# Add and gelu over 1024 x 4096 in fp32: larger rows, three adds on GpSimd, and another order on ScalarE

## The chip, the core and the metric

The kernel runs on one NeuronCore of a Trainium2 chip. The metric is the device time of one execution in microseconds (us). Before the change it was 120.32 us, the median of three runs (120.19 to 120.32).

## The reference

Two fp32 arrays `x` and `y` of 1024 x 4096 are added, and the tanh form of gelu is taken of the sum:

```python
z = x + y
return (0.5 * z * (1 + np.tanh(np.sqrt(2 / np.pi) * (z + 0.044715 * z ** 3)))).astype(np.float32)
```

Each of `x`, `y` and the output has 16.78 MB, so 50.33 MB go through the DMA engines.

## The kernel before

The arrays are seen as 128 partitions with 32768 elements each (L87). The tile `z` (L117) holds all 32768 elements per partition: `x` is loaded into it, the sums overwrite `x`, and the gelus overwrite the sums. The tile `y` (L118) has room for one half, 16384 elements; the second half of `y` goes into the same place as the first. So a load of the second half of `y` has to wait until the adds that read that part of the first half are done.

**Transfers.** All of them are issued by SyncE (SP), in the order of L158 to L160, and run through one queue on 16 DMA engines: the first half of `y`; the two halves of `x`; the second half of `y` in two pieces of 12288 and 4096 elements (`yloads`, L91); the two halves of the output (`stores`, L92). A piece of n elements is moved in 128 rows, one for each partition, of 4n bytes: 64 KB rows for a half, 48 KB and 16 KB rows for the two pieces. `begin_early` puts the first two loads ahead of the barrier with which the program starts. In the text below the transfers are called y1, x0, x1, y2 (with y3 where there is a second piece), store 0 and store 1.

**Work.** The 32768 elements are cut into chunks (L93), 15 of 2048 and at the end two of 1024. For each chunk VectorE adds `z` and `y` (L151), and ScalarE takes the gelu in place (L156). GpSimd and PSUM have no part in it (`by_pool` and `in_psum` are empty, L94 and L95), though the functions `to_psum` and `add` could use them.

**Order.** Lists for each queue (L158 to L166) say what each engine does and in what order; engines run their lists in that order, and waits on semaphores are put in where one operation needs another (`needs`, L168). ScalarE takes the gelus in the order of the chunks. Store 0 needs the gelus of the first half; these are long done when `y` of the second half is still on its way, so L133 to L139 add a wait on add 8 (`GATE = 8`, L96), the first add of the second half. Store 1 needs the gelus of the second half. The wait for store 1's end is the last thing in the program (`wait_late`).

Of the kernel before, what the change touches and what calls it, by code (L numbers as in the profile page):

```python
# [8 lines left out]
def begin_early(nc, count):  # L9


    head, body = (b.instructions for b in nc.main_func.blocks[:2])
    SP = mybir.EngineType.SP
    moved = [i for i in body if i.engine == SP and isinstance(i, mybir.InstDMACopy)][:count]
    assert not any(i.sync_info and i.sync_info.on_wait for i in moved)
    assert all(i.regs_accessed() == ((), ()) for i in moved)
    at = next(k for k, i in enumerate(head) if i.engine == SP)
    for k, i in enumerate(moved):
        body.remove(i)
        head.insert(at + k, i)  # L20


def wait_late(nc):

    body, end = (b.instructions for b in nc.main_func.blocks[1:3])
    last = [i for i in body if isinstance(i, mybir.InstDMACopy)][-1]
    (sem,) = [u.id for u in last.sync_info.on_update]
    all_done = end[0]  # L30
    reset = next(i for i in end if isinstance(i, mybir.InstDrain) and i.is_reset_sema)
    at = end.index(reset)
    clear = end[at + 1]
    first, stop = reset.reset_range_start, reset.reset_range_stop
    assert all_done.engine == mybir.EngineType.SP and reset.engine == mybir.EngineType.Pool
    assert isinstance(clear, mybir.InstISA) and clear.engine == mybir.EngineType.Pool
    waits = all_done.sync_info.on_wait
    (its,) = [w for w in waits if w.id == sem]

    end[0] = mybir.InstDrain(  # L40
        name=all_done.name, engine=all_done.engine, debug=all_done.debug, is_reset_sema=False,
        sync_info=mybir.SyncInfo(on_wait=[w for w in waits if w.id != sem], on_update=[]),
    )
    parts = []
    for f, e in ((first, sem), (sem + 1, stop)):
        if f < e:
            nc.gpsimd.sem_clear(range(f, e))
            parts.append(nc.cur_bb.bb.instructions.pop())
    end[at + 1 : at + 2] = parts
    end.append(  # L50
        mybir.InstEventSemaphore(
            name=clear.name, engine=mybir.EngineType.Activation, debug=clear.debug,
            sync_info=mybir.SyncInfo(
                on_wait=[its],
                on_update=[
                    mybir.SyncUpdate(
                        sync_type="semaphore", id=sem, ant_name=its.ant_name,
                        update_mode="sem-sub-imm", update_value=its.wait_value,
                    )
                ],  # L60
            ),
        )
    )


@with_exitstack
def kernel(
    ctx: ExitStack,
    tc: tile.TileContext,
    x: bass.AP,  # L70
    y: bass.AP,
    out: bass.AP,
):

    nc = tc.nc
    P = nc.NUM_PARTITIONS  # L80
    fp32 = mybir.dt.float32
    act = mybir.ActivationFunctionType

    N, D = x.shape
    assert N % P == 0
    TOT = N // P * D
    xv, yv, ov = (a.rearrange("(p n) d -> p (n d)", p=P) for a in (x, y, out))  # L87

    HALF = TOT // 2
    xloads = [HALF, HALF]  # L90
    yloads = [16384, 12288, 4096]  # L91
    stores = [16384, 16384]  # L92
    chunks = [2048] * 15 + [1024, 1024]  # L93
    by_pool = []  # L94
    in_psum = []  # L95
    GATE = 8  # L96

    def ranges(sizes):
        ends = [sum(sizes[: i + 1]) for i in range(len(sizes))]
        assert ends[-1] == TOT  # L100
        return [(e - f, e) for e, f in zip(ends, sizes)]

    xr, yr, sr, cr = (ranges(r) for r in (xloads, yloads, stores, chunks))
    C = len(cr)
    second = next(c for c in range(C) if cr[c][0] == HALF)

    def over(rs, lo, hi):
        return [i for i, (a, b) in enumerate(rs) if a < hi and b > lo]

    pool_sb = ctx.enter_context(tc.tile_pool(name="xz", bufs=1))  # L110
    pool_y = ctx.enter_context(tc.tile_pool(name="y", bufs=1))
    pool_ps = ctx.enter_context(
        tc.tile_pool(name="ps", bufs=max(1, len(in_psum)), space=bass.MemoryType.PSUM)
    )

    one = pool_sb.tile([P, 992], fp32, tag="one", name="one")
    zt = pool_sb.tile([P, TOT], fp32, tag="z", name="z")  # L117
    yt = pool_y.tile([P, HALF], fp32, tag="y", name="y")  # L118
    xp, adds = {}, {}

    def load_x(i):
        a, b = xr[i]
        nc.sync.dma_start(out=zt[:, a:b], in_=xv[:, a:b])

    def load_y(i):
        a, b = yr[i]
        o = a % HALF
        nc.sync.dma_start(out=yt[:, o : o + b - a], in_=yv[:, a:b])  # L128

    def store(i):  # L130
        a, b = sr[i]
        ins = nc.sync.dma_start(out=ov[:, a:b], in_=zt[:, a:b])
        if i == 0 and GATE is not None:  # L133
            tc.add_manual_dep(
                ins.ins,
                adds[GATE].name,
                mybir.DependencyInfo(mybir.DependencyClass.Sync, mybir.DependencyReason.DATA),
                reason="the stores join the queue when the last load is nearly done",
            )  # L139

    def to_psum(c):
        a, b = cr[c]
        xp[c] = pool_ps.tile([P, 2048], fp32, tag="xp", name=f"xp{c}")
        nc.scalar.copy(out=xp[c][:, : b - a], in_=zt[:, a:b])

    def add(c):
        a, b = cr[c]
        o = a % HALF
        eng = nc.gpsimd if c in by_pool else nc.vector
        first = xp[c][:, : b - a] if c in in_psum else zt[:, a:b]  # L150
        ins = eng.tensor_add(out=zt[:, a:b], in0=first, in1=yt[:, o : o + b - a])  # L151
        adds[c] = ins.ins

    def gelu(c):
        a, b = cr[c]
        nc.scalar.activation(out=zt[:, a:b], in_=zt[:, a:b], func=act.Gelu_apprx_tanh)  # L156

    sp = [(load_y, i) for i in over(yr, 0, HALF)] + [(load_x, 0), (load_x, 1)]  # L158
    sp += [(load_y, i) for i in over(yr, HALF, TOT)]
    sp += [(store, i) for i in range(len(stores))]  # L160
    pool = [(add, c) for c in by_pool]
    dve = [(add, c) for c in range(C) if c not in by_pool]
    order = list(range(second, C))
    acts = [(gelu, c) for c in range(second)] + [(to_psum, c) for c in in_psum]
    acts += [(gelu, c) for c in order]
    assert sorted(order) == list(range(second, C))  # L166

    needs = {  # L168
        load_x: lambda i: [],
        load_y: lambda i: [(add, c) for c in over(cr, yr[i][0] - HALF, yr[i][1] - HALF)],  # L170
        to_psum: lambda c: [(load_x, i) for i in over(xr, *cr[c])],
        add: lambda c: [(load_x, i) for i in over(xr, *cr[c])]
        + [(load_y, i) for i in over(yr, *cr[c])]
        + [(to_psum, k) for k in in_psum if k == c],
        gelu: lambda c: [(add, c)],
        store: lambda i: [(gelu, c) for c in over(cr, *sr[i])]
        + ([(add, GATE)] if GATE is not None else []),
    }
    queues = [sp, pool, acts, dve]
    done = set()  # L180
    with tc.manual_schedule():
        nc.vector.memset(one[:, :1], 0.0)  # L182
        nc.scalar.activation(out=one[:, :1], in_=one[:, :1], func=act.Gelu_apprx_tanh)  # L183
        while any(queues):
            moved = False
            for q in queues:
                while q and all(n in done for n in needs[q[0][0]](q[0][1])):
                    fn, arg = q.pop(0)
                    fn(arg)
                    done.add((fn, arg))  # L190
                    moved = True
                    if q is not sp:
                        break
            assert moved, [q[:1] for q in queues]

    ctx.close()
    tc.close()
    tc.compile()  # L198
    begin_early(nc, 2)
    wait_late(nc)  # L200
# [30 lines left out]
```

## Time and profile before

| What | Value |
|---|---|
| Median of three runs | 120.32 us (120.19 to 120.32) |
| The profiled execution | 120.19 us |
| Its span, from the first to the last instruction | 118.7 us |
| VectorE busy | 35.5 us, 17 adds and one memset |
| ScalarE busy | 32.0 us, 17 gelus, a table load and one small gelu |
| GpSimd busy | 0.2 us, four memsets |
| HBM read and written | 33.55 MB and 16.78 MB, 424 GB/s over the span |

In the tables of the profile, `L151 DVE` is line 151 of the kernel on VectorE; ACT is ScalarE, POOL is GpSimd, SPq is SyncE's queue. `out<-in` names the tiles. The span is shorter than the execution's time by what lies around it, 1.49 us here.

### The profile page before, as it was taken

What the parts mean: (1) busy time and instruction counts of PE and PEld (TensorE: products, weight loads), DVE (VectorE), ACT (ScalarE), POOL (GpSimd) and SP (SyncE); (2) the same over time, 40 slices, a digit from 0 to 9 for tenths busy, and PEclk for the clock granted to TensorE, in tenths of its full rate; (3) what the DMA queues carried; (4) which work ended last, traced back from release to release, by engine and by line L of the source; (5) the groups of instructions that cost most, each with busy time, mean ns of one, the idle gap of its engine ahead of it and who ended that gap; (6) DMA issues with size and microseconds to landing.
All of it is one profiled execution on the core that took longest, in us unless ns stands there. A gap on an engine that the chain in (4) does not pass through costs nothing.

```text
span 118.7 us, 96 instructions
## 1 busy us (share of the span) xinstructions
DVE 35.5 (30%) x18; ACT 32.0 (27%) x19; POOL 0.2 (0%) x4
## 2 busy tenths in 40 slices
DVE  0000000000000099999900000699999300000000
ACT  5000000000000029899850000079989800000000
POOL 0000000000000000000000000000000000000000
DMA  9889888998899888988898996998899889988890
GB/s 353 353 353 685 375 353 353 596 464 353 353 442 618 353 353 353 685 375 353 353 530 381 414 530 271 431 624 353 353 596 464 353 353 442 618 353 353 353 685 22
DMA packets 1008, 50.33 MB, mean 424 GB/s; under 512 B 112, under 2 KB 112, under 8 KB 112
## 3 DMA queue, kind: packets, MB, share of 16 engines
q1 hardware_dynamic: 1008, 50.33, 98.5%
HBM read 33.55 MB, written 16.78 MB: 424 GB/s over the span
## 4 chain that ended last, share of the span: by engine, by line
DMA 52%; DVE 22%; ACT 2%; DVEq 2%; ACTq 1%; SPq 0%; issue 0%
DMA z<-in_x_dram 34%; DVE z L151 22%; DMA y<-in_y_dram 17%; ACT z L156 2%; DVEq L198 2%; ACTq L198 1%; SPq L128 0%; DVEq L151 0%
## 5 line engine op out<-in xcount | busy, mean ns | idle before, releaser
L151 DVE TENSOR_TENSOR z<-z,y 128x2048 f32<-128x2048 f32 (+1 forms) x17 | 35.5, 2160 | 56.2 <-DMA z<-in_x_dram 40.0
L156 ACT ACTIVATE z<-z 128x2048 f32<-128x2048 f32 (+1 forms) x17 | 30.5, 1807 | 61.3 <-DVE z L151 61.3
L183 ACT ACT_TABLE_LOAD x1 | 1.3, 1283 | 1.3 <-PEq L215 1.3
L182 DVE MEMSET one<- 128x1 f32 x1 | 0.1, 59 | 1.3 <-PEq L215 1.3
L183 ACT ACTIVATE one<-one 128x1 f32<-128x1 f32 x1 | 0.2, 203 | 0.0
L215 POOL MEMSET const-bfloat16-1.0<- 128x1 bf16 x1 | 0.1, 101 | 0.0
L215 POOL MEMSET const-uint8-127<- 128x1 uint8 x1 | 0.1, 101 | 0.0
L215 POOL MEMSET const-float32-0.0<- 128x1 f32 x1 | 0.1, 98 | 0.2 <-issue 0.2
L215 POOL MEMSET const-float32-1.0<- 128x1 f32 x1 | 0.1, 98 | 0.0
## 6 DMA issues: line engine op xcount, KB each, us to landing
y<-in_y_dram SPq DMA_DIRECT2D x1, 6144.0 KB, 20.5
y<-in_y_dram SPq DMA_DIRECT2D x1, 2048.0 KB, 20.9
z<-in_x_dram SPq DMA_DIRECT2D x2, 50.1
out_dram<-z SPq DMA_DIRECT2D x2, 22.9
y<-in_y_dram SPq DMA_DIRECT2D x1, 22.0
```

The costliest lines, as they stand in the source:

```text
L151: ins = eng.tensor_add(out=zt[:, a:b], in0=first, in1=yt[:, o : o + b - a])
L156: nc.scalar.activation(out=zt[:, a:b], in_=zt[:, a:b], func=act.Gelu_apprx_tanh)
L182: nc.vector.memset(one[:, :1], 0.0)
L183: nc.scalar.activation(out=one[:, :1], in_=one[:, :1], func=act.Gelu_apprx_tanh)
L198: tc.compile()
L215: nc = _bacc.Bacc("TRN2", target_bir_lowering=False, num_devices=1)
```

## The change

The second half of `y` is loaded in one piece, so all six transfers have 64 KB rows. The wait on add 8 (`GATE`) is gone. The chunks are cut anew: the first half into two of 1024 (chunks 0 and 1) and seven of 2048 (2 to 8), the second half into 512, 1536 (9 and 10), six of 2048 (11 to 16), and 1024, 512, 512 (17 to 19). GpSimd does the adds of chunks 7, 8 and 12. ScalarE copies `x` of chunks 2 to 6 and 9 to 11 into PSUM, into a tile of 4096 elements (two places of 2048, or 512 + 1536 in the first), and VectorE's adds of these chunks take `x` from there; VectorE's other adds read both operands from SBUF as before. ScalarE's list is: the copies of 2 to 6, the gelu of 0, the copies of 9 to 11, then the gelus of 1 to 8, then those of 9, 10, 11, 13, 12, and 14 to 19. The copies of 9 to 11 need x1, and they stand ahead of the gelus of 1 to 8.

```diff
-    yloads = [16384, 12288, 4096]
+    yloads = [16384, 16384]
     stores = [16384, 16384]
-    chunks = [2048] * 15 + [1024, 1024]
-    by_pool = []
-    in_psum = []
-    GATE = 8
+    chunks = [1024, 1024] + [2048] * 7 + [512, 1536] + [2048] * 6 + [1024, 512, 512]
+    copies = {2: 0, 3: 2048, 4: 0, 5: 2048, 6: 0, 9: 0, 10: 512, 11: 2048}
+    on_vector = [0, 1, 2, 3, 4, 5, 6, 9, 10, 11, 13, 14, 15, 16, 17, 18, 19]
+    on_gpsimd = [7, 8, 12]
+    on_scalar = [("copy", c) for c in (2, 3, 4, 5, 6)] + [("gelu", 0)] + [("copy", c) for c in (9, 10, 11)] + [("gelu", c) for c in range(1, 9)] + [("gelu", c) for c in (9, 10, 11, 13, 12, 14, 15, 16, 17, 18, 19)]
...
+    ps = pool_ps.tile([P, 4096], fp32, tag="ps", name="ps")
...
+    def in_psum(c):
+        a, b = cr[c]
+        return ps[:, copies[c] : copies[c] + b - a]
...
     def store(i):
         a, b = sr[i]
-        ins = nc.sync.dma_start(out=ov[:, a:b], in_=zt[:, a:b])
-        if i == 0 and GATE is not None:
-            tc.add_manual_dep(
...
+        nc.sync.dma_start(out=ov[:, a:b], in_=zt[:, a:b])
+
+    def copy(c):
+        a, b = cr[c]
+        nc.scalar.copy(out=in_psum(c), in_=zt[:, a:b])

     def add(c):
         a, b = cr[c]
         o = a % HALF
-        eng = nc.gpsimd if c in by_pool else nc.vector
-        first = xp[c][:, : b - a] if c in in_psum else zt[:, a:b]
-        ins = eng.tensor_add(out=zt[:, a:b], in0=first, in1=yt[:, o : o + b - a])
-        adds[c] = ins.ins
+        eng = nc.gpsimd if c in on_gpsimd else nc.vector
+        first = in_psum(c) if c in copies else zt[:, a:b]
+        eng.tensor_add(out=zt[:, a:b], in0=first, in1=yt[:, o : o + b - a])
...
+    pool = [(add, c) for c in on_gpsimd]
+    dve = [(add, c) for c in on_vector]
+    acts = [(gelu if what == "gelu" else copy, c) for what, c in on_scalar]
...
-        store: lambda i: [(gelu, c) for c in over(cr, *sr[i])]
-        + ([(add, GATE)] if GATE is not None else []),
+        store: lambda i: [(gelu, c) for c in over(cr, *sr[i])],
```

## The prediction

> **What bounds the kernel now.** I read the page first, for who is busy. VectorE and ScalarE are busy for less than a third of the span. The DMA row of the 40 slices is full from end to end, and the one queue holds the 16 engines for 98.5% of the span:
>
> ```profile
> DMA  9889888998899888988898996998899889988890
> ...
> q1 hardware_dynamic: 1008, 50.33, 98.5%
> ```
>
> So time can be won only by moving the bytes in less engine time, and lost wherever an engine is left without a row. Next I asked for stretches of 1 us or less. The last two columns are the share of the 16 engines' time taken by rows that start in the stretch, and GB/s.
>
> ```profile
> 0.00:1.00 1.00, 0.00 (x0) 0.00 (x0) 0.20 (x4) 1.00 0.00 0
> 1.00:1.25 0.25, 0.00 (x0) 0.00 (x0) 0.00 (x0) 1.00 8.84 2884
> 1.25:1.50 0.25, 0.06 (x1) 0.24 (x1) 0.00 (x0) 1.00 2.88 1049
> 1.50:1.80 0.30, 0.00 (x0) 0.30 (x1) 0.00 (x0) 1.00 0.61 218
> ...
> 4.00:5.00 1.00, 0.00 (x0) 0.00 (x0) 0.00 (x0) 1.00 2.42 1049
> ...
> 63.00:64.00 1.00, 0.00 (x0) 0.00 (x0) 0.00 (x0) 1.00 1.82 786
> ...
> 76.00:77.00 1.00, 1.00 (x1) 0.00 (x0) 0.00 (x0) 1.00 1.11 475
> ```
>
> Two things are to be seen. First the **price of a row**: 1049 GB/s in 1 us is 16 rows of 64 KB, each taking 2.42 us; 786 is 16 rows of 48 KB at 1.82; 475 is 29 rows of 16 KB, at 1.11 x 16 / 29 = 0.61. Second the **price of a start**: y1 is issued at 0.00 and nothing moves for 1.00 us; 11 of the 16 engines begin by 1.25 (2884 GB/s x 0.25 us), the last between 1.50 and 1.80.
>
> Last the timeline and the landings give each transfer. Issue to landing is 22.0 for y1. x0 lands at 0.43 + 40.84 = 41.27 (chain of waits), x1 at 1.27 + 59.3 = 60.6, y2 at 54.70 + 20.47 = 75.17, y3 at 59.1 + 20.9 = 80.0. For the stores:
>
> ```profile
> L132 SPq DMA_DIRECT2D out_dram<-z x2: 343/346/348, 77.6 to 94.6; - x2
> ...
> DMA to landing us min/median/max: 21.7/22.9/24.0
> ```
>
> Store 0: 77.6 + 21.7 = 99.3; store 1: 94.6 + 24.0 = 118.6, the end. Between landings a half takes 19.3 us (41.27 to 60.6, 80.0 to 99.3, 99.3 to 118.6). Each transfer is issued well ahead of the landing of the one before it: store 0 by 80.0 - 77.6 = 2.4, store 1 by 99.3 - 94.6 = 4.7. I call this the **lead**. y1, before which nothing ran, took 22.0 - 19.3 = 2.7 more than a half. So a lead of 2.7 should always be enough, and store 0 shows that 2.4 is.
>
> **The change, part by part.**
>
> *Rows.* y2 and y3 give each engine 8 rows of 48 KB and 8 of 16 KB, 8 x (1.82 + 0.61) = 19.44; 8 rows of 64 KB are 8 x 2.42 = 19.36. The gain is 0.08 us, and it lies on the queue, so it counts in full. This is all that the change can win: bytes and engines stay. y2 then lands at 79.9 instead of y3's 80.0. One issue on SP (0.33) goes, hidden behind the queue.
>
> *First half.* VectorE's own row prices the adds, ScalarE's the copies:
>
> ```profile
> L151 DVE TENSOR_TENSOR z<-z,y 128x2048 f32<-128x2048 f32 x15 | 33.2, 2285 | 56.2 <-DMA z<-in_x_dram 40.0 <-DMA y<-in_y_dram 16.2
> L156 ACT ACTIVATE z<-z 128x2048 f32<-128x2048 f32 x15 | 28.6, 1910 | 61.3 <-DVE z L151 61.3
> L151 DVE TENSOR_TENSOR z<-z,y 128x1024 f32<-128x1024 f32 x2 | 2.4, 1219 | 0.0
> L156 ACT ACTIVATE z<-z 128x1024 f32<-128x1024 f32 x2 | 2.0, 1039 | 0.0
> ```
>
> Back to back an add of 2048 comes every 2.20 us (eight take 17.71 in the timeline) and, by the two shapes, 0.15 + 1.04 per 1000 elements; a gelu has 0.17 + 0.85 per 1000, and each of a run starts 0.09 before the last ends (3.80 for 1.91 + 1.04 + 1.04). From x0 at 41.3: VectorE's two adds of 1024 end at 43.7, the first copy at 43.3, and five adds from PSUM at 2.2 each end at 54.8. GpSimd's two adds run beside them. y2 is then issued at 54.9, a lead of 5.7 on x1. No cost. An add with one operand in PSUM and a copy into PSUM are not in the trace; the nearest rows are the same shapes above, which I take, with the fixed part (0.15, 0.17) gone or doubled as bounds.
>
> *Adds on GpSimd.* The trace has none. The floor is VectorE's 2.29. The one operation that both do is the memset of one column, 0.10 on GpSimd and 0.06 on VectorE, a ratio of 1.7, which makes 3.9 for 2048 elements; twice that, 7.8, is my ceiling, if it takes its two operands in turn. I take 3.9, by the row nearest to it. In the second half VectorE adds from PSUM until 84.5, and that covers 4.5 of chunk 12.
>
> The Trainium skill, "GPSIMD Engine Reference", section 3.1, gives 4497 ns for such an add and advises VectorE for elementwise work. By it the add just fits its cover, and the sum stays. No run here shows it yet.
>
> *ScalarE's order, store 0.* The copies of 9 to 11 wait for x1 and hold the gelus of 1 to 8 behind them, and store 0 waits for those. x1 lands at 60.6, ScalarE starts 0.1 later; copies 0.51 + 1.38 + 1.82; gelu 1 0.95; seven gelus 12.72; 0.09 for the last one's end: 78.2. The lead on y2 (79.9) is 1.7, where it was 2.4. Bounds of the copies: 0.5 either way.
>
> *Second half, store 1.* Before, three quarters of the work could start at 75.2. Now all of it starts at 79.9, that is 4.7 later. VectorE: chunk 9 from 80.0 to 80.7, 10 to 82.4, 11 to 84.6, 13 to 86.8, then one every 2.2. ScalarE follows: gelu 9 at 80.8, 10 at 82.4, 11 at 84.6 to 86.55; gelu 13 waits for its add and starts at 86.85; from there it is never without work: 13, 12, 14, 15, 16 at 1.82, 17 at 0.95, 18 at 0.51, and 19 with 0.60 end at 98.0. ScalarE is the later engine (VectorE is done at 95.8). Store 1 is issued at 98.0; without a hole store 0 would land at 99.2. The lead falls from 4.7 to **1.2**.
>
> *What a short lead costs.* This is the disputed price. Say that a store needs a lead L for no hole; then store 1 lands at 98.0 + L + 19.3. Ceiling of L: 2.4, by store 0 before. Floor: 0, if the queue had its rows ready at once. Nearest row: the start of y1, where the last engine got its first row 1.5 to 1.8 after the issue. I take L = 2.1, the middle of 1.8 and 2.4. Then store 1 lands at 119.4. Store 0's own hole (2.1 - 1.7 = 0.4) adds nothing to that, since store 1's issue is later still. The span goes from 118.7 to 119.5 (0.04 from landing to the last instruction), and with 120.19 - 118.7 = 1.49 around it the time is **121.0**. That is against the profiled 120.19; the median, 120.32, is 0.13 higher, which I leave to the range.
>
> The Trainium skill, "DMA: Bandwidth & Descriptors", section "Latency and other measured facts", has about 600 ns to the first byte of a transfer issued from SyncE. The row here is 1.00 to 1.80. With 0.6 in place of L there is no hole and the sum is 120.1.
>
> **Rivals.**
>
> *No hole (not slower).* Place: the end of store 0, at 99.2. If store 1's rows reach the engines within 1.2 us of its issue, the queue stays full and only the 0.08 remains: 120.1, or 120.25 on the median's side. It decides at L = 1.2. For it: the first 11 engines started within 1.25 at the very start, when SP's instruction itself (0.38) was slower than a store's 0.34. Against it: the last one came after 1.50, and the end is set by the last engine.
>
> *GpSimd in VectorE's way.* The Trainium skill, "SBUF — State Buffer", section "Who interferes with whom", says that a VectorE add with both operands in SBUF and a GpSimd add that reads SBUF exclude each other, whichever comes second waiting to the end. No row here shows both engines at work.
>
> Whatever the reason, if GpSimd's add stood between VectorE's chunks 0 and 1, VectorE would end the first half 3.9 later, at 58.7, still a lead of 1.9 on x1, with a cost of 0.2; behind both, it ends at 62.6, y2 is issued 2.0 after x1 has landed, and all behind it moves by 2.0 + 2.1: about 125. With the ceiling of 7.8 for chunk 12, store 1 is issued 3.3 later: 124.3. For this: the two engines are released by the same landing. Against: VectorE's two such adds are only 2.3 us long.
>
> *Faster by more than the rows.* The queue has 1.5% unused, 1.8 us, nearly all of it the start that stays. There is no row that shows more to win: below 120.08 I see nothing but luck.
>
> **How the numbers follow.** A measurement tells about 0.2% (0.24 us) from no change. Hole at store 1: 0.55, with L from 1.8 to 2.7 and the issue 0.4 to either side, 120.6 to 121.9. No hole, or one under 0.3: 0.27, 120.1 to 120.5. GpSimd in the way: 0.13, 122 to 125. Faster: 0.05. Range: the first two cases, 0.82, 120.1 to 121.9. Slower 0.55 + 0.13 = 0.68; same 0.27; faster 0.05.
>
> **What would show it.** Right: y2 lands at 79.9; SP issues store 1 at 97.6 to 98.4; issue to landing is 21.1 to 22.0 for store 1; the DMA row has a dent near 99. Wrong: landings of the stores still 19.3 apart (no hole); y2 issued after 58 or VectorE idle beside GpSimd at 41 to 44 (the lock); ScalarE done before 97 (my chain of gelus too long).

## The result, and the profile after

The changed kernel takes 122.73 us (median of four runs, 122.53 to 122.91), the kernel before 120.25 in the same comparison. The ratio is 1.0218, 95% interval 1.0205 to 1.0232: 2.2% slower. The profiled execution took 122.53 with a span of 121.0, that is 1.5 around it as before.

The page of the changed kernel, the lines that answer to those of before:

```profile
DMA  9799779977998899779989879988998888997792
...
q1 hardware_dynamic: 864, 50.33, 97.3%
```

The queue still holds the engines nearly all the time. But 2.7% of the longer span is 3.3 us without a row, where 1.5% was 1.8: that is 1.5 of the 2.3 us by which the span grew. The rest, 0.8, lies in rows that took longer, as will be seen. The holes do not stand out in the slices of 3 us. The transfers show them. Of the changed kernel, SP's instructions for `y` and the output (first and last start at the end of each line) and the time from issue to landing:

```profile
L134 SPq DMA_DIRECT2D y<-in_y_dram x2: 327/350/373, 0.0 to 59.0; - x2
...
DMA to landing us min/median/max: 21.9/22.5/23.1
```

```profile
L138 SPq DMA_DIRECT2D out_dram<-z x2: 344/346/348, 78.0 to 100.2; - x2
...
DMA to landing us min/median/max: 20.8/22.2/23.5
```

y2 is issued at 59.05 (the forecast: 54.9) and lands 23.1 later, at 82.1. x1 landed at 60.5 and a half takes 19.3, so y2 is 2.3 later than a full queue would have it, and 2.1 later than y3 landed before. Store 0, issued at 78.0 while y2 is under way, lands at 78.0 + 23.5 = 101.5, that is 19.3 after y2 (101.45 - 82.13): no hole. Store 1, issued at 100.2, lands at 121.0, 19.5 after store 0: a hole of 0.2. So 2.1 + 0.2 = 2.3, the whole growth of the span (121.0 - 118.7). All but 0.2 of it is the late landing of y2.

Why y2 was issued so late stands in the timeline of the changed kernel around x0's landing (start, duration, engine, and in brackets the idle time before):

```profile
41.24 3.67 ACT L142 COPY ps<-z 128x2048 f32<-128x2048 f32 x2 [38.48 <-DMA z<-in_x_dram]
41.31 6.66 DVE L149 TENSOR_TENSOR z<-z,y 128x1024 f32<-128x1024 f32 x2 [39.93 <-DMA z<-in_x_dram]
41.35 11.00 POOL L149 TENSOR_TENSOR z<-z,y 128x2048 f32<-128x2048 f32 x2 [40.92 <-DMA z<-in_x_dram]
47.90 11.07 DVE L149 TENSOR_TENSOR z<-ps,y 128x2048 f32<-128x2048 f32 x5
...
59.05 0.33 SPq L134 DMA_DIRECT2D y<-in_y_dram  x1
```

VectorE's two adds of 1024 take 6.66 instead of 2.3. The durations of each line's instructions tell how (minimum, median, maximum in ns):

```profile
L149 DVE TENSOR_TENSOR z<-z,y x9: 685/2282/5521, 41.3 to 97.3; 128x2048 f32<-128x2048 f32 x4, 128x1024 f32<-128x1024 f32 x3, 128x512 f32<-128x512 f32 x2
L149 DVE TENSOR_TENSOR z<-ps,y x8: 692/2276/2282, 47.9 to 84.5; 128x2048 f32<-128x2048 f32 x6, 128x512 f32<-128x512 f32 x1, 128x1536 f32<-128x1536 f32 x1
L149 POOL TENSOR_TENSOR z<-z,y x3: 4529/5496/5538, 41.4 to 82.3; 128x2048 f32<-128x2048 f32 x3
```

One add of 1024 with both operands in SBUF (chunk 1) took 5.5 us, where 1.2 is its own price. GpSimd's adds took 5.5 in the first half and 4.53 in the second, where VectorE beside it had `x` in PSUM. VectorE's adds from PSUM never exceed 2.28. This fits an exclusion by turns: chunk 0 on VectorE, GpSimd's chunk 7 waiting about 1.0 and then running 4.5, chunk 1 on VectorE waiting through that, GpSimd's chunk 8 waiting for chunk 1. VectorE's five adds from PSUM start 4.2 later than 43.7, and the first half ends at 58.97.

### The profile page after: what moved, and what is told of

Same layout as the page of the kernel before. It is cut to its first block, busy times and chain, and to the rows that moved or that the text cites. A ratio compares the mean times of both kernels' runs of the same rounds, so it can differ in the third digit from the quotient of the medians.

```text
span 121.0 us, 112 instructions
## 1 busy us (share of the span) xinstructions
DVE 33.4 (28%) x18; ACT 44.2 (37%) x30; POOL 15.7 (13%) x7
## 4 chain that ended last, share of the span: by engine, by line
DMA 53%; DVE 19%; ACT 8%; DVEq 1%; ACTq 1%; SPq 0%; issue 0%
DMA z<-in_x_dram 34%; DMA y<-in_y_dram 19%; DVE z L149 19%; ACT z L153 8%; DVEq L196 1%; ACTq L196 1%; SPq L134 0%; DVEq L149 0%
## 5 line engine op out<-in xcount | busy, mean ns | idle before, releaser
L153 ACT ACTIVATE z<-z 128x2048 f32<-128x2048 f32 (+3 forms) x20 | 29.8, 1556 | 7.1 <-DVE z L149 7.1
L142 ACT COPY ps<-z 128x2048 f32<-128x2048 f32 (+2 forms) x8 | 13.0, 1654 | 47.6 <-DMA z<-in_x_dram 41.6
L149 DVE TENSOR_TENSOR z<-z,y 128x2048 f32<-128x2048 f32 (+2 forms) x9 | 17.9, 2053 | 39.9 <-DMA z<-in_x_dram 39.9
L149 POOL TENSOR_TENSOR z<-z,y 128x2048 f32<-128x2048 f32 x3 | 15.5, 5188 | 70.8 <-DMA z<-in_x_dram 40.9
L149 DVE TENSOR_TENSOR z<-ps,y 128x2048 f32<-128x2048 f32 (+2 forms) x8 | 15.6, 2013 | 23.3 <-DMA y<-in_y_dram 23.3
```

The source lines that it names most:

```text
L142: nc.scalar.copy(out=in_psum(c), in_=zt[:, a:b])
```

## The experiments

All kernels compute the whole function. Each kernel's comparison is with the kernel before, on the same chip and at the same time (120.04 in the first set, 120.08 in the two others).

**Theory A**: the two engines exclude each other, so y2 is issued late, and a load that joins late costs far more than the forecast had it. **Rivals**: GpSimd's or PSUM's traffic, or the size of y2, slows the transfers; or the hole is at the stores. In the texts below that were written before each run, "the lock" is this exclusion.

### E1: chunks 0 and 1 through PSUM too

```diff
-    copies = {2: 0, 3: 2048, 4: 0, 5: 2048, 6: 0, 9: 0, 10: 512, 11: 2048}
+    copies = {0: 0, 1: 1024, 2: 2048, 3: 0, 4: 2048, 5: 0, 6: 2048, 9: 0, 10: 512, 11: 2048}
-    on_scalar = [("copy", c) for c in (2, 3, 4, 5, 6)] + [("gelu", 0)] + ...
+    on_scalar = [("copy", c) for c in range(7)] + [("gelu", 0)] + ...
```

> Chunks 0 and 1 are copied into PSUM too, so no VectorE add beside GpSimd reads two operands from SBUF. Theory A (the two engines shut each other out, VectorE ends its first half late, y2 is issued only 1.5 us ahead of x1's landing and a load needs a lead of about 3.6): GpSimd's adds take 4.5 instead of 5.5, VectorE ends near 56.0, y2 is issued near 56.1 with a lead of 4.4 and lands at 79.9; store 1's lead is 1.3 as in the changed kernel and costs 0.2; time 120.3. Rival B (the late landing of y2 comes from GpSimd's or PSUM's traffic beside the transfers, or from its size, not from its issue): y2 lands after 81.5 again, time 122 or more. Rival C (the recorded forecast: a store needs a lead of 2.1): y2 lands at 79.9, but store 1 loses 0.8, time 121.0.

Measured: 120.16, ratio 1.0012 (0.9997 to 1.0026). The timeline of E1 in the same place:

```profile
41.23 9.02 POOL L149 TENSOR_TENSOR z<-z,y 128x2048 f32<-128x2048 f32 x2 [40.79 <-DMA z<-in_x_dram]
42.16 2.36 DVE L149 TENSOR_TENSOR z<-ps,y 128x1024 f32<-128x1024 f32 x2 [40.78 <-ACT ps L142]
44.91 11.08 DVE L149 TENSOR_TENSOR z<-ps,y 128x2048 f32<-128x2048 f32 x5 [0.39 <-ACT ps L142]
...
56.07 0.33 SPq L134 DMA_DIRECT2D y<-in_y_dram  x1
```

VectorE waits 0.8 for the first copy, but then nothing stands in its way: 2.36 for the two adds, 9.02 for GpSimd's two instead of 11.00. y2 is issued 3.0 earlier and lands at 56.1 + 23.8 = 79.9. With that the 2.5 us are gone. GpSimd's and PSUM's work is still all there, and y2 is as large: rival B falls. So does the forecast's own hole: store 1 has the same lead of 1.3 and still lands at 97.9 + 20.7 = 118.6.

### E2: no GpSimd in the first half

```diff
-    on_vector = [0, 1, 2, 3, 4, 5, 6, 9, 10, ...
+    on_vector = [0, 1, 2, 3, 4, 5, 6, 7, 8, 9, 10, ...
-    on_gpsimd = [7, 8, 12]
+    on_gpsimd = [12]
```

> Chunks 7 and 8 go back to VectorE, with both operands in SBUF; GpSimd keeps chunk 12 alone. No engine is in another's way in the first half, but VectorE has all of it and ends near 59.0, so y2 is issued as late as in the changed kernel. Theory A: y2 lands near 82.1 again and the time is 122.7, as with the two adds on GpSimd. Rival B, if GpSimd's adds disturb the transfers: y2 lands near 80.5, time about 121.

Measured: 122.70, ratio 1.0203 (1.0180 to 1.0227), as slow as the changed kernel with no two engines in each other's way: VectorE's adds of 1024 with both operands in SBUF take 1.22 each here, with no add on GpSimd beside them. y2 is issued at 58.95 and lands 23.7 later, at 82.6. It is the late issue that costs, whatever makes it late.

### E3 and E9: the price of a load's lead

E3 is E1 with chunk 7 on VectorE too, its `x` copied into PSUM like the others; E9 also moves 1024 elements from that chunk to GpSimd's chunk 8. Against the changed kernel:

```diff
-    copies = {2: 0, 3: 2048, ...
+    copies = {0: 0, 1: 1024, 2: 2048, 3: 0, 4: 2048, 5: 0, 6: 2048, 7: 0, 9: 2048, 10: 2560, 11: 0}
-    on_vector = [0, 1, 2, 3, 4, 5, 6, 9, ...
+    on_vector = [0, 1, 2, 3, 4, 5, 6, 7, 9, ...
-    on_gpsimd = [7, 8, 12]
+    on_gpsimd = [8, 12]
-    on_scalar = [("copy", c) for c in (2, 3, 4, 5, 6)] + ...
+    on_scalar = [("copy", c) for c in range(8)] + ...
# E9 besides:
-    chunks = [1024, 1024] + [2048] * 7 + ...
+    chunks = [1024, 1024] + [2048] * 5 + [1024, 3072] + ...
```

> As the kernel with all of VectorE's first-half adds in PSUM, but GpSimd takes chunk 8 alone there, so VectorE ends near 58.2 and y2 has a lead of 2.3. Theory A, with the lead of 3.6 that the changed kernel shows: y2 lands 1.3 late, at 81.2, time 121.7. Rival (a load needs no more than the 2.4 that a store was shown to be content with): y2 lands at 80.0, time 120.4. Rival B: after 81.5, time 122 or more.

> As the kernel with one chunk on GpSimd in the first half, but that chunk has 3072 elements and VectorE's share 1024 fewer, so y2 is issued near 57.3, a lead of 3.2 on x1's landing (2.1 lost 2.5 us, 4.5 lost nothing). Theory A1 (a load needs its first rows on the engines before x1's last rows begin, 3.1 before the landing: a threshold): y2 lands at 79.9, time 120.2. Rival A2 (the loss shrinks evenly with the lead): y2 lands near 81.2, time 121.4.

Measured: E3 122.95, ratio 1.0234 (1.0213 to 1.0255); E9 121.06, ratio 1.0081 (1.0054 to 1.0108). I missed E3's time: a lead of 2.1 loses as much as one of 1.5. Of the two theories for E9 the threshold at 3.1 falls; an even shrinking is not borne out either (0.8 lost where it gives 1.3, and 2.1 no better than 1.5). No lead between 3.2 and 4.5 was tried. In the profiled executions:

| Kernel | y2 issued | Lead on x1 | y2 lands | Later than with a full queue |
|---|---|---|---|---|
| E1 | 56.1 | 4.5 | 79.9 | 0.0 |
| E9 | 57.3 | 3.2 | 80.7 | 0.8 |
| E3 | 58.4 | 2.1 | 82.4 | 2.5 |
| changed kernel | 59.05 | 1.5 | 82.1 | 2.3 |
| E2 | 58.95 | 1.4 | 82.6 | 2.9 |

The last column holds all that y2 loses; a part of it turns out below to be lost at its end and not by its lead. What happens at the start can be seen in the stretch in which the 16 engines take y2's first rows. Changed kernel first, then E1 (the columns as in the prediction):

```profile
59.90:61.40 1.50, 0.00 (x0) 0.80 (x2) 0.00 (x0) 1.00 2.01 699
```

```profile
59.40:61.40 2.00, 0.00 (x0) 0.79 (x2) 0.00 (x0) 1.00 1.21 524
```

Both hold 16 rows of 64 KB (699 x 1.5 and 524 x 2.0 make 1049). A row takes 2.01 x 1.5 = 3.02 in the changed kernel and 1.21 x 2.0 = 2.42 in E1. So besides starting late the first rows are 0.6 longer, like those of y1 at the start of the program (3.11). A store that joins a queue gone dry is not like that. The changed kernel's store 1:

```profile
100.90:101.40 0.50, 0.00 (x0) 0.00 (x0) 0.00 (x0) 1.00 4.90 2097
```

All 16 rows begin 0.7 to 1.2 after the issue at 100.16 and take 4.90 x 0.5 = 2.45.

### E4 and E5: the gelus before the copies

On ScalarE the gelus of 1 to 8 stand ahead of the copies of 9 to 11, in the changed kernel (E4) and in E1 (E5). This undoes what I call the hold: copies that wait for x1 keep those gelus, and with them store 0, back.

```diff
-    on_scalar = ... + [("copy", c) for c in (9, 10, 11)] + [("gelu", c) for c in range(1, 9)] + ...
+    on_scalar = ... + [("gelu", c) for c in range(1, 9)] + [("copy", c) for c in (9, 10, 11)] + ...
```

> The changed kernel with the gelus of chunks 1 to 8 ahead of the copies of 9 to 11 on ScalarE, so store 0 is issued near 71 instead of 78.0; the lock in the first half stays. Theory A: y2's lateness is made at its start, it lands near 82.1, time 122.7. Rival D (y2's last rows, 2.9 to 3.1 us on the three last engines instead of 2.42, are slowed because store 0 joins the queue while they are under way): those rows take 2.42, y2 lands near 81.4, time 122.0. Rival E (a store that joins early disturbs the loads): y2 lands later than 82.1, time 123 or more.

> The kernel without the lock (all of VectorE's first-half adds beside GpSimd take x from PSUM), and the gelus of chunks 1 to 8 ahead of the copies of 9 to 11, so store 0 is issued near 72 and stands in the queue while y2 runs; y2 has its lead of 4.4. Theory D (a store that is queued behind a load slows the load's last row on every engine, by 1.5 us when it stands there for the whole row): y2's last rows take 3.5 to 4.2, it lands near 81.3, store 1 is issued as much later, time 121.6. Rival (slow last rows are a sequel of the hole at y2's start, which this kernel has not): y2 lands at 79.9, time 120.2.

Measured: E4 123.75, ratio 1.0312 (1.0280 to 1.0344); E5 121.29, ratio 1.0083 (1.0060 to 1.0105). So the hold is worth about 1 us in either kernel (0.9 to 1.1 by the ratios). In E4 y2 lands at 58.9 + 24.5 = 83.4, as its rival E has it. For the queue E5 differs from E1 only in when store 0 is issued (68.2 instead of 78.0). y2 lands at 56.2 + 24.9 = 81.1 instead of 79.9. Here are y2's last 16 rows, in E1 and in E5:

```profile
76.45:77.15 0.70, 0.00 (x0) 0.70 (x1) 0.00 (x0) 1.00 3.46 1498
```

```profile
76.40:77.20 0.80, 0.00 (x0) 0.00 (x0) 0.00 (x0) 1.00 4.37 1311
```

In E1 they take 3.46 x 0.7 = 2.42, in E5 4.37 x 0.8 = 3.50. A store that is queued behind a load stretches the load's last rows. That is theory D. The expectation for E4, which put y2's whole lateness at its start, was wrong, and so was its rival D, by which a store that joins earlier leaves the last rows at 2.42: they take 3.81 in E4.

### E7: store 0 after y2's landing

```diff
+        if i == 0:
+            tc.add_manual_dep(ins.ins, adds[9].name, ...)
...
-        store: lambda i: [(gelu, c) for c in over(cr, *sr[i])],
+        store: lambda i: [(gelu, c) for c in over(cr, *sr[i])] + [(add, 9)],
```

> The changed kernel, but store 0 also waits for add 9, the first that needs y2, so no store is in the queue while y2 runs. Theory D: y2's last rows take 2.42 and it lands at 81.4 instead of 82.1; store 0 is issued 0.9 after that, and with the 1.5 that a store takes to start it lands near 103.1 and store 1 near 122.5: time 124.0. Rival: the last rows stay at 2.5 to 3.1, y2 lands at 82.1, time 124.7.

Measured: 124.06, ratio 1.0309 (1.0281 to 1.0337), the time that theory D gives. The profiled execution, at 124.75 the longest of the four, has y2 landing at 82.3, as the rival has it, but not for the rival's reason: its last rows take 2.46 on average, only three of them over 2.48, and nearly all that is lost is lost before them: the last of these rows begins at 79.4, in E1 at 77.1. In the changed kernel the last rows are these:

```profile
77.50:78.80 1.30, 0.00 (x0) 0.44 (x1) 0.00 (x0) 1.00 2.00 807
```

All 16 have begun by 78.8 and take 2.00 x 1.3 = 2.60 on average, the three that begin last 2.9 to 3.1. So of y2's 2.3 in that execution 1.6 were lost at the start (78.7 against 77.1) and 0.6 in the last rows, behind which store 0 already stood. The hold was timed for a y2 that lands at 79.9; as y2 came later, store 0 stood behind it for longer. The profiled executions put in order by that:

| Kernel | Store 0 issued ahead of y2's landing | The last of y2's last 16 rows begins | Their mean duration |
|---|---|---|---|
| E7 | not ahead | 79.4 | 2.46 |
| E1 | 1.9 | 77.1 | 2.42 |
| E9 | 2.7 | 77.9 | 2.43 |
| changed kernel | 4.2 | 78.7 | 2.60 |
| E3 | 4.4 | 78.8 | 2.75 |
| E2 | 4.8 | 78.7 | 2.80 |
| E4 | 12.5 | 78.8 | 3.81 |
| E5 | 13.0 | 77.2 | 3.50 |

A late start with no store behind the load (E7) leaves nearly all its last rows at 2.42; a store behind it without a late start (E5) does not. By this table the short lead alone costs y2 0.8 us at 3.2 ahead of x1's landing (E9) and 1.6 to 2.3 at 1.4 to 2.1 (the changed kernel, E2, E3, E4 and E7). E7 shows a store's own price too: store 0 was issued at 83.2, 0.9 after y2 had landed, and landed 20.7 later, so a store needs a lead of 20.7 - 19.3 = 1.4.

### E8: the kernel before, without its wait

```diff
-    GATE = 8
+    GATE = None
```

> The kernel before with GATE = None: store 0 is issued near 61, as soon as the first half's gelus are done, and stands in the queue while y2 (48 KB rows) and y3 (16 KB rows) run. No row of the change is in it. Theory D (a store queued behind a load slows the load's last rows, by an amount that does not shrink with the row): y3's 16 KB rows take up to 1.6 instead of 0.61, y3 lands near 80.9, time 121.1. Rival D2 (the slowing is in proportion to the row, so it matters only with the change's 64 KB rows): y3 lands near 80.3, time 120.4. Rival (the wait was not needed here): 120.1.

Measured: 121.03, ratio 1.0066 (1.0048 to 1.0084). y3, issued at 59.0, lands 22.0 later at 80.9, where it was 80.0. The 32 of its rows that start between 77.20 and 78.95 take 1.02 each on average instead of 0.61. So the stretching is nearly as large with 16 KB rows in the last load (0.9 against the 1.2 of E5), and the wait on add 8 was worth 0.8 us in the kernel before. The hold is what takes its place.

### E10: y2 in two pieces again

```diff
-    yloads = [16384, 16384]
+    yloads = [16384, 12288, 4096]
```

> The changed kernel with the second half of y in two pieces of 12288 and 4096 again, so the last load has 16 KB rows; the lock stays, and both pieces are issued near 59. Theory A with D: the hole at the start stays (1.3 to 1.5 us), but the store that joins finds only rows of a quarter of the length: y3 lands near 81.5, VectorE starts on the first piece at 76.6, so store 1 is issued in good time; time 121.6. Rival (it is the lead of y2 alone, the last rows do not matter): y3 lands at 82.1, time 122.3.

Measured: 123.11, ratio 1.0238 (1.0199 to 1.0277), no better than the changed kernel. Chunk 6, the last add on VectorE, holds up the first piece as it held up the whole, and the last piece lands at 59.2 + 23.4 = 82.6. My expectation that short last rows would spare some time fell here; E8, which ran after this, agrees.

### E6: E1 with the last store in two

```diff
-    stores = [16384, 16384]
+    stores = [16384, 12288, 4096]
```

> The kernel without the lock, with the last store in two pieces of 12288 and 4096, so the first piece is issued near 94.4, ahead of the end of store 0 by 4.8 instead of 1.3. The hole in front of store 1, worth 0.07 there, goes; the smaller rows cost 0.08. Theory: 120.1, no difference from the kernel before within 0.2%. Rival: the second piece, issued near 97.9, still finds a busy queue and the whole is 0.2 faster: 119.9.

Measured: 120.14, ratio 0.9997 (0.9979 to 1.0015). Neither E1 nor E6 beats the kernel before: with the queue full, neither order has won anything.

## Why the prediction was wrong, point by point

- *Slower.* That was forecast, but for a hole at store 1, and that hole measured 0.2 us of the 2.3. Without the exclusion in the first half the same plan takes 120.16 (E1), a ratio of 1.0012 (0.9997 to 1.0026). So the direction came true by luck; the "no hole" rival (0.27) was right about store 1.
- *The bound.* Right. The queue is the whole time, and each loss was a stretch in which engines lacked rows or rows were long. The gain of 0.08 for 64 KB rows is too small to be seen in a time; E1, with those rows, is at 1.0012.
- *First half: "GpSimd's two adds run beside them. y2 is then issued at 54.9, a lead of 5.7 on x1. No cost."* This is the step that failed. Beside VectorE's adds of 1024 they do not run: VectorE's first half ended at 58.97, y2 was issued at 59.05 with a lead of 1.5, and it landed 2.3 late. That is the prediction's own sign of the lock, y2 issued after 58. The rule that speaks against it, in the Trainium skill, "SBUF — State Buffer", section "Who interferes with whom", I had quoted and given a chance of 0.13. The runs agree with it: 5.5 us for an add of 1.2 us where both engines read two operands from SBUF, 2.28 and 4.53 us for adds of 2048 side by side where VectorE has one in PSUM.
- *The rival's price: "still a lead of 1.9 on x1, with a cost of 0.2".* The delay of VectorE was right (58.7; measured 58.97), the price was not. I took the lead that a store needs for the one that a load needs. y2 came 2.3 to 2.9 late at leads of 1.4 to 2.1 (1.6 to 2.3 of it at its start, the rest in its last rows), and 0.8 late at 3.2. So "a lead of 2.7 should always be enough" is wrong for a load. By the prediction's own sum this case came to about 121 (121.0 + 0.2); with 2.3 for the 0.2 it would have come to about 123. That the rival's range, 122 to 125, holds the measured 122.73 is luck too: it was drawn for its other cases, at 124.3 and 125.
- *Store 1: "I take L = 2.1".* Too large. Store 1 came with the lead forecast (1.3 against 1.2) and lost 0.2, in E1 0.1; a store needs 1.4. The nearest row that I took, y1's start, was that of a load, with rows that began 1.0 to 1.8 after the issue; store 1's began 0.7 to 1.2 after it.
- *Issue times.* Right: store 0 at 78.0 (78.2), and store 1 18.0 after y2's landing (98.0 - 79.9 = 18.1).
- *GpSimd's add.* 4.53 where nothing held it up; I took 3.9 within 2.29 and 7.8. The Trainium skill's 4497 ns ("GPSIMD Engine Reference", section 3.1) was nearer than my row.
- *The hold.* I counted it as a cost (a lead of 1.7 in place of 2.4). It cost nothing and saves about 1 us: the lead of store 0 has to be short, and that was in no step of mine.

## What to carry to other kernels

Where a DMA queue sets the time, price each transfer by how far ahead of the end of the one before it is issued, and do so for loads and stores apart: here a load lost 0.8 us at a lead of 3.2 and nothing at 4.5, and a store needed 1.4. A store should join behind a load late: here 1.9 to 2.7 us ahead of the load's landing cost the load nothing, 4.2 and more did. And before two engines are set to work side by side, look at what each reads: here an add on GpSimd ran beside VectorE's only where VectorE had one operand in PSUM.

## What the runs showed of the hardware that I had not expected

- A load that joins a nearly dry queue starts with long rows, 3.02 us for 64 KB instead of 2.42; a store's first rows took 2.45.
- A store queued behind a load lengthens the load's last rows, from 2.42 to 3.50 us for 64 KB (E5); a load whose last piece has 16 KB rows landed 0.9 us later (E8). The reason was not found, nor why a lead of 2.1 costs a load as much as one of 1.5.
